# Three rings of buffers around the feed-forward up products of a one-core transformer layer

## The chip, the cores and the metric

The kernel runs on one core of a Trainium2 chip. A core has TensorE (PE in the profile, its weight loads PEld), VectorE (DVE), ScalarE (ACT), GpSimd (POOL) and SyncE (SP), each with its own queue of instructions that it works through in order. The metric is the device time of one execution in microseconds; before and after are compared by their medians.

## The reference

One layer of a diffusion backbone on 2048 latent tokens and 128 context tokens, width 1024: modulated norm, an attention and a convolution branch, an output projection, and then a feed-forward part. Only the last one is touched here:

```python
def finish_layer(x, ao, co, gate_a, shift_f, scale_f, gate_f,
                 w_out, g_attn_post, g_ffn_pre, g_ffn_post, w_ffn_in, w_ffn_out):
    mix = jnp.concatenate([ao, co], axis=-1) @ w_out
    x = x + gate_a * rms_norm(mix, g_attn_post)
    u = rms_norm(x, g_ffn_pre) * (1.0 + scale_f) + shift_f
    gu = u @ w_ffn_in
    h = jax.nn.silu(gu[..., :D_FF]) * gu[..., D_FF:]
    return x + gate_f * rms_norm(h @ w_ffn_out, g_ffn_post)
```

D_FF is 2816, so `u @ w_ffn_in` is (2176 x 1024) by (1024 x 5632). The time before is 3061.99 us.

## The kernel before

**Up products.** The 17 row tiles of 128 tokens (16 latent, number 16 the context) are dealt into three chunks of 5, 6 and 6 tiles. The chunks are worked one after another, each over 22 blocks of the hidden width. One chunk and one block make a unit (`up_unit`): a Strassen-like scheme with seven products in place of eight, over pairs of row tiles. Each product takes 4 contraction steps, and each factor is split into a high and a low part, so a step is three matmuls (lines 957 to 959) and a unit 84, with 320 columns in chunk 0 and 384 in chunks 1 and 2.

**Weight operands.** For each unit two raw tiles of 512 KB are loaded (`wi_raw`, tag `t4`, four buffers). `wi_ops` forms four sums of quarter weights on GpSimd, each in a buffer `st` (line 919), and splits seven operands: ScalarE casts the high part (line 81), VectorE subtracts it for the low part (line 82). The split tiles `wi` lie in three `km` buffers and one `qt`, which come free as TensorE ends the products of the unit before. The sums follow one from another: s2 from s1, s4 from s2.

**Row operands.** The seven operands of chunk 0 (`u_ops`) are built ahead, during the output projection (`build_kept`), and kept. Those of chunks 1 and 2 are built in the middle of the chunk before (`build_spilled`), one pair of tiles after units 2, 8 and 14: six builds in all. `build_tile` loads a row tile `row` (line 834, tag `t4` as the raw weights), scales it on GpSimd (line 836), transposes it in eight matmuls (line 842) into PSUM banks of tag `c`, and copies these out on ScalarE (line 843). `build_pair` makes seven operands of two tiles, four of them by differences on GpSimd (`td`, line 860). Each is split into `hl` on ScalarE and VectorE and written to HBM (`u2d`, 512 KB). At the end of a chunk the operands of the next are read back (`u<-u2d`, 1.5 MB each); two of them already during the third build.

**What sets the order.** The instructions are traced in program order, and a scheduler puts them into one order for each engine, by a timeline of its own and by when buffers come free. So a ring of buffers that is longer also changes the order around it. All DMAs are issued from SP's queue. A tile's buffer is taken again when everything that reads it is done; for `hl` that is the landing of its write to HBM.

Of the kernel before, what the change touches and what calls it, by code (L numbers as in the profile page):

```python
# [8 lines left out]
F32 = mybir.dt.float32  # L9
F32R = mybir.dt.float32r  # L10
# [7 lines left out]
P = 128  # L18
D = 1024
# [21 lines left out]
def layer(ctx, tc, x_prompt, x_sample, cache_k, cache_v, cond, w_ada, b_ada, gcol,  # L41
# [28 lines left out]
    def dma(out, in_):  # L70

        out, in_ = (x.bitcast(F32) if x.dtype == F32R else x for x in (out, in_))
        with tc.issue_after(behind[0]) if behind else ExitStack():
            return nc.sync.dma_start(out, in_).ins
# [4 lines left out]
    def split(h, l, src, eng=None):  # L79

        S.copy(h, src)  # L81
        (eng or V).tensor_tensor(l, src, h.bitcast(F32), op=ALU.subtract)  # L82
# [20 lines left out]
    def pool(name, **kw):  # L103
        st = ExitStack()
        return st, st.enter_context(tc.tile_pool(name=name, reuse_waits="tile", **{"bufs": 1, **kw}))
# [574 lines left out]
    def t4(name):  # L680
        return prow.tile([P, D], F32, tag="t4", name=name, bufs=4)
# [142 lines left out]
    x_ex, bld = pool("extra", side="left")  # L824
# [6 lines left out]
    def build_tile(ti, bank):  # L831

        c = int(ti == 16)
        row = t4("row")
        dma(row, x2d[ti])
        G.tensor_scalar(row, row, r2s[:, ti:ti + 1], 1.0, op0=ALU.mult, op1=ALU.mult)
        ur = bld.tile([P, KT, P], F32, tag="ur", name="ur", bufs=2)
        for kk in range(2):
            up = bank().rearrange("p (a t) -> p a t", t=P)
            for a in range(4):  # L840
                kt = 4 * kk + a
                T.transpose(up[:, a, :], row[:, kt * P:(kt + 1) * P], ident)
                S.activation(ur[:, kt, :], up[:, a, :], AF.Identity, scale=modc[:, 2, c, kt:kt + 1],
                             bias=modc[:, 3, c, kt:kt + 1])
        return ur

    def build_pair(pair, bank, out):

        if len(pair) == 2:
            ua, ub_ = (build_tile(ti, bank) for ti in pair)  # L850
            w = P
        else:
            ur = build_tile(pair[0], bank)
            ua, ub_ = ur[:, :, 0:64], ur[:, :, 64:128]
            w = 64
        b11, b12, b21, b22 = ua[:, 0:4], ub_[:, 0:4], ua[:, 4:8], ub_[:, 4:8]

        def diff(x, y):
            t = bld.tile([P, 4, P], F32, tag="td", name="td", bufs=2)[:, :, :w]
            G.tensor_tensor(t, x, y, op=ALU.subtract)  # L860
            return t

        out(0, w, b11)
        out(3, w, b21)
        out(5, w, b22)
        t = diff(b12, b11)
        out(1, w, t)
        t2_ = diff(b22, t)
        out(2, w, t2_)
        out(6, w, diff(b21, t2_))  # L870
        out(4, w, diff(b22, b12))
# [38 lines left out]
    x_sm, sm_ = pool("small", side="right")  # L910
    x_ex, bld = pool("build", side="right")
    x_psg, psg = pool("psg", space=PSUM, bufs=2)

    def wi_ops(raws):
        a11, a12, a21, a22 = (r[:, i * 512:(i + 1) * 512] for r in raws for i in range(2))

        def total(x, y, op):
            t = sm_.tile([P, 512], F32, tag="st", name="st", bufs=2)
            G.tensor_tensor(t, x, y, op=op)  # L919
            return t  # L920

        dst = []
        for k in range(4):
            if k < 3:
                km = pk.tile([P, NALL], F32R, tag="km", name="wi", bufs=3)
                dst += [(km[:, 1024 * q:1024 * q + 512], km[:, 1024 * q + 512:1024 * q + 1024]) for q in range(2)]
            else:
                q = pk.tile([P, 2, 512], F32R, tag="qt", name="wi", bufs=2)
                dst.append((q[:, 0], q[:, 1]))
        split(*dst[0], a11)  # L930
        s1 = total(a21, a22, ALU.add)
        split(*dst[1], s1)
        s2 = total(s1, a11, ALU.subtract)
        split(*dst[2], s2)
        split(*dst[3], a12)
        s3 = total(a11, a21, ALU.subtract)
        split(*dst[4], s3)
        s4 = total(a12, s2, ALU.subtract)
        split(*dst[5], s4)
        split(*dst[6], a22)  # L940
        return dst
# [4 lines left out]
    def bank(tag):  # L946
        return psg.tile([P, 512], F32, tag=tag, name="psg")
# [51 lines left out]

    def build_spilled(c, k):  # L1000
        def out(i, w, src):
            hl = bld.tile([P, 2, 4, P], F32R, tag="hl", name="hl", bufs=1)
            split(hl[:, 0, :, :w], hl[:, 1, :, :w], src)
            dma(u2d[c, i][:, :, :, k * P:k * P + w], hl[:, :, :, :w])

        build_pair(chunks[c][k], lambda: bank("c"), out)
# [6 lines left out]
    for c in range(3):  # L1013
# [18 lines left out]
        elif c == 1:  # L1032
            u_ops = nxt + [u_load(pua, i, 2) for i in (2, 3)] + [u_load(pub, i, 2) for i in (4, 5, 6)]
            x_ex.close()
            x_ex, bld = pool("down", side="right")
# [33 lines left out]
    for gn, (c, g) in enumerate(groups):  # L1069
# [3 lines left out]
        for f in range(NF):  # L1073
# [9 lines left out]
            for i in range(len(tiles)):  # L1083
                hh, hl = (hhl[:, s, i * P:(i + 1) * P] for s in range(2))
# [75 lines left out]
```

## Time and profile before

| what | us |
|---|---|
| three runs | 3058.20, 3061.99, 3064.18 |
| median | 3061.99 |
| profiled execution, its time | 3067.98 |
| its span | 3066.2 |
| TensorE busy in the span | 2909.8 |
| chunk 0 of the up products | 1548 to 1862 |
| chunk 1 | 1862 to 2218 |
| chunk 2 | 2218 to 2538 |
| six builds of spilled operands | within 1594 to 2175 |

The profile's page gives busy time by engine, the chain of work that ended last, and groups of instructions by line with the idle time before them and what ended it. Other views give the same for a window, list who waited for whom, or show one tile's instructions. A wait is put down to what ended last.

### The profile page before, as it was taken

The numbers are of one execution on the slowest core, as the hardware profiler recorded it, in microseconds if no ns is written. First come the engines' busy times: TensorE is split into PE (matmuls) and PEld (weight loads), VectorE is DVE, ScalarE is ACT, GpSimd is POOL, SyncE is SP. The second block draws the span as 40 slices with busy tenths as digits, with TensorE's granted clock in tenths as the row PEclk, the third lists the DMA queues.
The fourth block names the chain that finished last, engine by engine and source line by source line (L and its number), as shares of the span: only waits on it lengthen the run. The fifth ranks groups of instructions, "written<-read, shape, count | busy, mean of one in ns | idle before, by whom it ended". The sixth has DMA issues, their size and how long they took to land. (4 is left out here: it accounts for less than half of the span.)

```text
span 3066.2 us, 47162 instructions
## 1 busy us (share of the span) xinstructions
PE 2909.8 (95%) x16925; PEld 2653.8 (87%) x16925; DVE 1994.7 (65%) x3824; ACT 1444.4 (47%) x2651; POOL 1230.1 (40%) x1114
## 2 busy tenths in 40 slices
PE   4999989999999999999999999999999999999998
PEld 3778879999999999988889988999999998788886
DVE  7899568787787887863366765556655554554443
ACT  3323236565565565664445553544444443444442
POOL 7313125554545544532245654555444440111110
PEclk7999999999999999999999999999999999999999
DMA  7777564454454454457645565444633235766663
GB/s 250 244 251 247 171 198 129 137 173 123 138 168 128 132 159 124 114 162 224 196 140 152 154 200 195 150 147 153 227 136 101 96 103 199 238 220 218 220 220 118
DMA packets 351180, 525.25 MB, mean 171 GB/s; under 512 B 33089, under 2 KB 264673, under 8 KB 349153
## 3 DMA queue, kind: packets, MB, share of 16 engines
q1 hardware_dynamic: 350944, 522.23, 53.7%
q8 instruction: 133, 2.18, 0.3%
q14 instruction: 103, 0.84, 0.1%
HBM read 393.79 MB, written 128.34 MB: 170 GB/s over the span
## 5 line engine op out<-in xcount | busy, mean ns | idle before, releaser
L957 PE MATMUL psg<-u,wi 128*128 128x384 f32 (+1 forms) x1848 | 606.6, 331 | 28.4 <-ACT wi L81 11.6
L959 PE MATMUL psg<-u,wi 128*128 128x384 f32 (+1 forms) x1848 | 597.6, 329 | 9.8 <-DVE wi L82 9.8
L958 PE MATMUL psg<-u,wi 128*128 128x384 f32 (+1 forms) x1848 | 606.2, 328 | 0.0
L505 DVE TENSOR_SCALAR_CACHE_REDUCE e<-s 128x436 f32<-128x436 f32 (+2 forms) x648 | 373.4, 600 | 87.1 <-PE s L502 70.7
L957 PEld LDWEIGHTS psg<-u,wi 128*128 128x128 f32 x1848 | 349.6, 190 | 38.6 <-ACT wi L81 15.5
L959 PEld LDWEIGHTS psg<-u,wi 128*128 128x128 f32 x1848 | 348.1, 189 | 13.9 <-DVE wi L82 13.5
L502 PE MATMUL s<-km,qt 128*128 128x436 f32 (+1 forms) x1280 | 344.1, 372 | 13.2 <-DVE e L505 9.1
L82 DVE TENSOR_TENSOR wi<-st,wi 128x512 fp32r<-128x512 f32 x264 | 246.1, 935 | 160.8 <-ACT wi L81 157.0
L958 PEld LDWEIGHTS psg<-u,wi 128*128 128x128 f32 x1848 | 350.1, 189 | 0.3
L82 DVE TENSOR_TENSOR wo<-rawo,wo 128x1024 fp32r<-128x1024 f32 x132 | 167.0, 1265 | 252.3 <-ACT wo L81 252.3
L510 ACT ACTIVATE e<-e,nm 128x2176 f32<-128x2176 f32 (+1 forms) x136 | 273.9, 2014 | 78.2 <-DVE nm L509 77.3
L81 ACT CAST wi<-st 128x512 fp32r<-128x512 f32 x264 | 163.3, 619 | 279.6 <-PE psg L959 190.8
L1089 PE MATMUL psy<-wo,hhl 128*128 128x512 f32 x748 | 286.0, 391 | 1.8 <-DVE hhl L82 1.8
L1088 PE MATMUL psy<-wo,hhl 128*128 128x512 f32 x748 | 286.5, 390 | 0.9 <-DVE wo L82 0.9
L1087 PE MATMUL psy<-wo,hhl 128*128 128x512 f32 x748 | 286.2, 391 | 0.0
L81 ACT CAST wo<-rawo 128x1024 fp32r<-128x1024 f32 x132 | 139.1, 1054 | 294.3 <-PE psy L1089 284.1
L82 DVE TENSOR_TENSOR wi<-raw,wi 128x512 fp32r<-128x512 f32 x198 | 233.0, 1193 | 35.5 <-ACT wi L81 30.7
L502 PEld LDWEIGHTS s<-km,qt 128*128 128x128 f32 x1280 | 209.1, 190 | 26.1 <-DVE e L505 17.5
L81 ACT CAST ath<-t 128x512 fp32r<-128x512 f32 (+2 forms) x292 | 157.4, 555 | 114.9 <-PE t L546 107.6
L82 DVE TENSOR_TENSOR atl<-t,ath 128x512 fp32r<-128x512 f32 (+2 forms) x292 | 187.1, 649 | 36.4 <-ACT ath L81 35.7
L1060 POOL TENSOR_TENSOR rr<-rr,mhalf 128x1 f32<-128x1 f32 x17 | 13.1, 779 | 452.7 <-DVE rr L1059 452.7
L919 POOL TENSOR_TENSOR st<-raw,st 128x512 f32<-128x512 f32 x66 | 87.3, 1322 | 254.4 <-DVE wi L82 254.4
(264 smaller groups left out, 7040.5 us busy)
## 6 DMA issues: line engine op xcount, KB each, us to landing
raw<-in_w_fi SPq DMA_DIRECT2D x132, 512.0 KB, 4.2
rawo<-in_w_fo SPq DMA_DIRECT2D x132, 512.0 KB, 3.6
fu<-ud SPq DMA_DIRECT2D x256, 256.0 KB, 4.7
raw<-in_w_ada SPq DMA_DIRECT2D x48, 512.0 KB, 5.2
u2d<-hl SPq DMA_DIRECT2D x42, 512.0 KB, 3.9
u<-u2d SPq DMA_DIRECT2D x14, 1536.0 KB, 10.7
hr<-hid SPq DMA_DIRECT2D x110, 192.0 KB, 3.5
hid<-hid SPq DMA_DIRECT2D x88, 192.0 KB, 3.6
```

The lines of the kernel that those rows point to most:

```text
L81: S.copy(h, src)
L82: (eng or V).tensor_tensor(l, src, h.bitcast(F32), op=ALU.subtract)
L502: mm = T.matmul(ps[:, :n], qt[:, s, m, t * P:(t + 1) * P], km[m][:, k0:k0 + n], start=(s == 0), stop=(s == 1))
L505: V.tensor_scalar(et[:, k0:k0 + n], ps[:, :n], SCALE, None, op0=ALU.mult, op1=ALU.max, accum_out=mx[:, ci:ci + 1])
L510: S.activation(et[:, :nk], et[:, :nk], AF.Exp, bias=nm, scale=1.0, accum_out=sm[:, t, m:m + 1])
L919: G.tensor_tensor(t, x, y, op=op)
L957: T.matmul(ps, h[:, ks], u[:, 0, kt, :n], start=start and kt == 0, stop=False, skip_group_check=not start)
L958: T.matmul(ps, h[:, ks], u[:, 1, kt, :n], start=False, stop=False, skip_group_check=not start)
L959: T.matmul(ps, l[:, ks], u[:, 0, kt, :n], start=False, stop=kt == 3, skip_group_check=not start)
L1087: T.matmul(banks[i][:, b, :], hh, woh_[:, bs], start=(f == 0), stop=False)
L1088: T.matmul(banks[i][:, b, :], hh, wol_[:, bs], start=False, stop=False)
L1089: T.matmul(banks[i][:, b, :], hl, woh_[:, bs], start=False, stop=(f == NF - 1))
```

## The change

Three allocations differ. The row tile gets a tag of its own in the pool of the builds, with one buffer, in place of one of the four `t4`. `st` has three buffers in place of two. `hl` has two in place of one. Every instruction stays, with the same sizes.

```diff
     def build_tile(ti, bank):

         c = int(ti == 16)
-        row = t4("row")
+        row = bld.tile([P, D], F32, tag="row", name="row")
         dma(row, x2d[ti])
...
         def total(x, y, op):
-            t = sm_.tile([P, 512], F32, tag="st", name="st", bufs=2)
+            t = sm_.tile([P, 512], F32, tag="st", name="st", bufs=3)
             G.tensor_tensor(t, x, y, op=op)
...
     def build_spilled(c, k):
         def out(i, w, src):
-            hl = bld.tile([P, 2, 4, P], F32R, tag="hl", name="hl", bufs=1)
+            hl = bld.tile([P, 2, 4, P], F32R, tag="hl", name="hl", bufs=2)
             split(hl[:, 0, :, :w], hl[:, 1, :, :w], src)
             dma(u2d[c, i][:, :, :, k * P:k * P + w], hl[:, :, :, :w])
```

The order moves on all engines from the first `build_tile` to the end of the builds. On ScalarE, in the second build of chunk 0, the fourth and fifth casts of `hl` stood like this before (`sg` and `u` are the gate's SiLU, `p` and `psg` copies of PSUM that the next products wait for):

```order
L81 CAST wi<-raw_19934 128x512
L81 CAST hl<-td 128x512
L976 ACTIVATE sg<-psg 128x320
L81 CAST wi<-st 128x512
L968 COPY psg<-psg 128x320
L983 ACTIVATE u_20020<-u_20020 128x320
L81 CAST wi<-st 128x512
L81 CAST wi<-raw_20071 128x512
L81 CAST hl<-td 128x512
```

and the fifth and sixth stand like this now:

```order
L971 COPY p_19965<-psg 128x320
L81 CAST wi<-st 128x512
L81 CAST hl<-td 128x512
L81 CAST wi<-raw_20069 128x512
L81 CAST hl<-td 128x512
L81 CAST wi<-st 128x512
L81 CAST wi<-raw_19934 128x512
```

Two casts of `hl` have one instruction between them instead of seven; the third and fourth of a build stand side by side. Counted in TensorE's matmuls that ScalarE's queue has waited for by then, the casts of tiles 3, 5 and 7 of a build lie 35 and 24 apart in chunk 0 (first and third build), and 21 and 39 in chunk 1 (first and second build).

On SP, around the loads of the row tiles for the second build of chunk 0 (x2d_119 and x2d_111 are the rows of tiles 16 and 8), before:

```order
L74 DMA row<-x2d_119 128x1024
L74 DMA hid_7_16913<-hid 128x256
L74 DMA hid_7_16913<-hid 128x64
L74 DMA row<-x2d_111 128x1024
L74 DMA hid_7_16913<-hid 128x256
L74 DMA hid_7_16913<-hid 128x64
L74 DMA raw_19795<-in_w_fi 128x1024
L74 DMA raw_19797<-in_w_fi 128x1024
```

Now x2d_119 is loaded during the build before it. x2d_111 comes within its own build, between the raw weights and the first writes of `hl`, and the first row of the next build (x2d_109) shortly behind it:

```order
L74 DMA u2d_18780<-hl 1024x1x128
...
L74 DMA raw_20069<-in_w_fi 128x1024
L74 DMA row<-x2d_111 128x1024
L74 DMA u2d_18783<-hl 1024x1x128
L74 DMA raw_20071<-in_w_fi 128x1024
L74 DMA row<-x2d_109 128x1024
L74 DMA u2d_18785<-hl 1024x1x128
L74 DMA u2d_18781<-hl 1024x1x128
```

Both rows stood ahead of the raw weights; now the second row of a pair is loaded when the first has been transposed. On TensorE the last transpose of the first row and the first of the second have 55, 41 and 55 matmuls of the products between them in the three builds of chunk 0, and 40, 36 and 60 in those of chunk 1.

## The prediction

> **What bounds the kernel now.** I read the page's busy line first, then stretches of the up products, then the waits of TensorE in the worst of them, then the tile that is named there.
>
> ```profile
> span 3066.2 us, 47162 instructions
> PE 2909.8 (95%) x16925; PEld 2653.8 (87%) x16925; DVE 1994.7 (65%) x3824; ACT 1444.4 (47%) x2651; POOL 1230.1 (40%) x1114
> ```
>
> TensorE is the bound: only what fills its 156 us of idle time, or what it waits for, can move the end. The change acts from the first rows built to the end of the up products, so I cut that part into stretches (window: length, PE busy with count, PEld, DVE, ACT, POOL, clock, DMA share, GB/s):
>
> ```profile
> 1380.00:1545.00 165.00, 165.00 (x746) 135.37 (x745) 58.90 (x81) 75.96 (x180) 38.16 (x47) 1.00 0.65 202
> 1594.08:1654.04 59.96, 53.60 (x351) 50.74 (x350) 42.52 (x48) 31.97 (x68) 34.28 (x24) 1.00 0.61 178
> 1679.15:1738.67 59.52, 53.75 (x350) 52.09 (x349) 44.02 (x49) 31.36 (x67) 34.34 (x24) 0.97 0.61 179
> 1763.66:1824.80 61.14, 54.91 (x352) 52.29 (x350) 40.61 (x49) 32.02 (x68) 34.45 (x24) 0.97 0.71 221
> 1824.80:1849.44 24.64, 24.64 (x171) 24.64 (x169) 16.18 (x20) 12.02 (x25) 13.71 (x10) 1.00 0.39 119
> 1899.84:1968.45 68.61, 63.26 (x354) 59.65 (x353) 41.51 (x50) 34.75 (x73) 36.62 (x27) 1.00 0.53 158
> 1997.57:2080.14 82.57, 77.94 (x437) 75.76 (x437) 50.93 (x57) 40.11 (x83) 42.95 (x30) 0.98 0.48 145
> 2094.70:2174.25 79.55, 75.96 (x437) 74.32 (x437) 50.94 (x59) 41.36 (x86) 43.27 (x30) 1.00 0.64 198
> 2174.25:2217.93 43.68, 43.68 (x253) 43.68 (x253) 25.10 (x32) 18.50 (x36) 20.61 (x15) 1.00 0.54 193
> 2217.93:2538.00 320.07, 320.07 (x1848) 320.07 (x1848) 174.31 (x219) 136.37 (x263) 146.31 (x108) 1.00 0.35 116
> ```
>
> Rows 2 to 4 are the three builds of spilled operands in chunk 0, rows 6 to 8 those in chunk 1; rows 5 and 9 are units without a build, the last is chunk 2, which builds nothing. Without a build TensorE never pauses, and the pace is 24.64/171 = 0.144 us a matmul in chunk 0 and 43.68/253 = 0.173 us in chunk 1. At that pace the six builds would take 50.6, 50.4, 50.7, 61.1, 75.4 and 75.4 us. They take 9.4, 9.1, 10.4, 7.5, 7.1 and 4.1 us more: **47.6 us**, the most that this change can take from its own stretches. The first row, with the kept operands, has no idle time, so nothing is to be won there. TensorE's waits from 1594 to 2175 us:
>
> ```profile
> PE psg L957 <- ACT psg L968: 9.1, 10, 1.7
> PE psg L959 <- DVE wi L82: 8.9, 12, 1.6
> PE psg L957 <- ACT wi L81: 8.7, 8, 3.2
> ```
>
> These three, 26.7 us, are a copy and splits that ACT and DVE deliver late. The tile hl says why they are late:
>
> ```profile
> L81 ACT CAST hl<-td x24: 617/622/625, 1621.3 to 2162.0; 128x512 fp32r<-128x512 f32 x24
> L82 DVE TENSOR_TENSOR hl<-td,hl x24: 675/692/1785, 1622.4 to 2162.7; 128x512 fp32r<-128x512 f32 x24
> ...
>   DMA u2d<-hl: 75.7, 29
> ...
> DMA to landing us min/median/max: 3.5/3.9/10.4
> ```
>
> With one buffer each cast of hl waits until the tile before it has landed in HBM: a cycle of 0.62 + 0.69 + 3.9 = 5.2 us, in which ACT, which works in order, does nothing else. It stood 75.7 us at these casts. One such wait, on ACT and then on TensorE:
>
> ```profile
> 1783.53 0.62 ACT L81 CAST wi<-st 128x512 fp32r<-128x512 f32 x1 [0.54 <-POOL st L919]
> 1790.95 0.62 ACT L81 CAST hl<-ur 128x512 fp32r<-128x512 f32 x1 [6.80 <-DMA u2d<-hl]
> 1791.48 0.42 ACT L971 COPY p<-psg 128x320 f32<-128x320 f32 x1
> 1791.79 0.62 ACT L81 CAST wi<-raw 128x512 fp32r<-128x512 f32 x1
> ...
> 1792.47 0.42 PE L957 MATMUL psg<-u,wi 128*128 128x320 f32 x1 [3.23 <-ACT wi L81]
> ```
>
> The weight cast that TensorE wants stands behind the hl cast; it comes 6.8 us late and TensorE stops for 3.2 us. After some stops the clock falls too:
>
> ```profile
> 1711.00:1717.90 6.90, 4.73 (x33) 4.46 (x31) 5.24 (x6) 3.19 (x7) 6.20 (x5) 1.00 0.85 258
> 1717.94:1721.35 3.41, 3.41 (x13) 3.33 (x14) 3.41 (x4) 2.08 (x5) 2.09 (x3) 0.50 0.56 158
> 1721.35:1724.76 3.41, 3.41 (x25) 3.41 (x24) 2.31 (x3) 1.00 (x2) 1.42 (x1) 1.00 0.40 112
> ```
>
> 13 matmuls instead of 25 in 3.41 us: about 1.6 us are lost each time, and this belongs to the 47.6. Here 6.90 - 4.73 = 2.2 us of idle time in the stretch ahead sufficed for it.
>
> **The change part by part.** No instruction is added or removed; three rings of buffers and the order differ.
>
> *Second hl buffer.* Cast k now waits for the landing of tile k-2. In the new order tiles 3 and 4 go side by side, and 5 and 6 follow. Counted in matmuls, tile 5 stands 35 behind tile 3 in chunk 0 (35 x 0.144 = 5.0 us, needed 5.2: held 0.2 us) and tile 7 stands 24 behind tile 5 (3.5 us: held 1.7). In chunk 1 it is 21 (3.6 us: held 1.6) and 39 (6.7 us: nothing held). That is 1.9 and 1.6 us a build, 10 us for six. In the third build of each chunk 1.5 MB operand loads share the DMA engines and a landing took up to 10.4 us, 6.5 more than the median; I keep one of these for each of the two, 13 us. So ACT is held 23 us in place of 75.7, 30%, and if TensorE's loss falls alike, 14 to 15 of the 47.6 us stay: **-33 us**. Bounds: all of it (-47.6), or, if landings go to 10.4 us throughout, a cycle of 11.7 us against those spacings: 6.7 + 8.2 us a build in chunk 0 and 8.1 + 5.0 in chunk 1, 84 us held as before, gain 0.
>
> *Own tile for the row, and third st.* What they touch:
>
> ```profile
> L919 POOL TENSOR_TENSOR st<-raw 128x512 f32<-128x512 f32 x38 | 58.0, 1525 | 22.4 <-DMA raw<-in_w_fi 20.9
> L919 POOL TENSOR_TENSOR st<-raw,st 128x512 f32<-128x512 f32 x38 | 50.8, 1338 | 94.1 <-DVE wi L82 94.1
> ...
> L836 POOL TENSOR_SCALAR row<-row,r2s x11: 1122/1492/2088, 1590.1 to 2101.9; 128x1024 f32<-128x1024 f32 x11
> ...
> DMA to landing us min/median/max: 3.1/3.5/4.5
> ```
>
> POOL's fourth sum waits 94.1 us for DVE, as the two st are taken; the third ends that wait. Raw weights no longer share t4 with rows, so the 20.9 us of waits for them should shrink. Chunk 2 runs with two st and no pause, so neither binds TensorE outside the builds, and inside they work through the same late splits: cost 0 by themselves, between -6 (part of the 8.9 us on DVE's splits) and the loss of the second rival. What the row pays: its second tile loads only after the first is transposed. Between the two sets of transposes the new order has 55, 41, 55 matmuls in chunk 0 and 40, 36, 60 in chunk 1, so 7.9, 5.9, 7.9, 6.9, 6.2 and 10.4 us, for a landing of 3.5 and a scaling of 1.5: 5.0 us, covered by 0.9 to 5.4 us. For the kept operands the same serial load lies under projection matmuls with no idle time: 0.
>
> **Sum.** 3066.2 - 33 = 3033.2 us of span, and with the 1.8 us that the profiled execution has around it 3035. Its own time, 3067.98, is 6.0 us above the median 3061.99, so the forecast for a median is **3029 us**.
>
> **The rivals.**
> *Landings still pace the casts* (0.20). For it: pairs of 512 KB writes go out together, beside raw loads, and a landing without any operand load has taken 6.65 us already:
>
> ```profile
> 1629.46 6.65 DMA u2d<-hl
> ```
>
> Then the cycle is 8.0 us, the holds 3.0 + 4.5 us a build in chunk 0 and 4.4 + 1.3 in chunk 1, 40 for six, 53 with the operand loads: 70% of 75.7 stay, gain 14, 3048 us. Against it: DMA is busy 0.48 to 0.71 of the builds.
> *The second row comes late* (0.08), the slower side. The first transposes of the second row stand in TensorE's order; behind them everything waits. The scaling stands on POOL behind a sum that waits for DVE. At 6 us for that wait, the path is 3.5 + 6 + 1.3 + 1.5 = 12.3 us against the spacings above: short by 4.4, 6.4, 4.4, 5.4, 6.1 and 1.9, 28.6 us, and six half-clock spells of 1.6 bring 38. Against the gain of 33 that is 5 slower, 3067. It decides from a mean lateness of 3.9 us (6 x (3.9 + 1.6) = 33). Against it: the fourth sum waits only 94.1/38 = 2.5 us, and the third st is what shortens this.
> *DVE and POOL in each other's way* (0.05). DVE's subtraction takes 0.69 us in the median and up to 1.79 (row of hl). If the freed POOL made all seven splits of a chunk 0 unit take 1.79, they need 12.5 us of the unit's 12.1 (84 x 0.144) before any other DVE work; with 1.4 us of PSUM reads 13.9, 1.8 over, times 22 units 40 us, less the gain 7 slower: 3069. It decides from (12.1 - 1.4)/7 = 1.53 us a split. The splits and one of the three reads:
>
> ```profile
> L82 DVE TENSOR_TENSOR wi<-st,wi 128x512 fp32r<-128x512 f32 x171 | 176.5, 1036 | 83.7 <-ACT wi L81 80.5
> ...
> L979 DVE TENSOR_TENSOR c<-psg,p 128x320 f32<-128x320 f32 x22 | 10.6, 483 | 3.1 <-PE psg L959 2.4 <-ACT p L971 0.7
> ```
>
> The mean of 1.04 us is far from 1.53. The Trainium skill (SBUF — State Buffer, SBUF: two separate sides) calls the port of the two engines an exclusive lock, held for the whole instruction when DVE reads two SBUF operands; the trace agrees in kind, 0.69 alone and up to 1.79, but POOL's amount of work stays the same.
> *The buffers change nothing* (0.05): the order already shows two hl casts side by side, so only if the late splits had another cause. 3060.
>
> **How the numbers follow.** Forecast 0.62, gain 20 to 47 us, 3015 to 3042. The first rival, 3048 with some 7 us either way, reaches 3055; a full recovery (47.6) and 5 us of the waits outside the builds, where raw weights also share t4, end at 3009. What lies outside is the slower cases and half of no change: range 3009 to 3056. A change of 0.2%, 6 us, is about what can be told from none. Faster: the forecast, the first rival, and 0.02 of the row case where lateness is smaller than the gain, 0.84. Same: 0.05 and some 0.02 of rivals that just cancel, 0.07. Slower: 0.09.
>
> **What would show it.** ACT's wait for u2d<-hl falls from 75.7 us to about 23 and the six stretches lose some 33 us of their 47.6; POOL's wait for DVE at the fourth sum all but goes. TensorE's wait for POOL's row (L842 <- row L836) stays near 0; if it shows 10 us or more the row rival is at work. DVE's mean at wi above 1.2 us would show the port. The forecast fails if ACT's hold falls and TensorE's idle time does not.

## The result, and the profile after

| | median us | runs | range |
|---|---|---|---|
| before | 3062.06 | 8 | 3058.20 to 3066.70 |
| after | 3080.94 | 8 | 3071.69 to 3088.87 |

The ratio is 1.0056, with a 95% interval of 1.0043 to 1.0070: the change makes the kernel **slower by 0.56%**, where 1.1% faster was forecast, 3029 us with a range of 3009 to 3056. The profiled execution after took 3071.69 us, the fastest of its eight, so its trace shows less of the loss than the median has.

The page of the changed kernel, its first two lines:

```profile
span 3069.9 us, 47302 instructions
PE 2907.6 (95%) x16925; PEld 2655.4 (86%) x16925; DVE 1944.0 (63%) x3824; ACT 1437.3 (47%) x2651; POOL 1236.8 (40%) x1114
```

VectorE is busy for less time in total than before (1944.0 us against 1994.7), and ScalarE no longer stands at the casts of hl. The view of that tile after:

```profile
L82 DVE TENSOR_TENSOR hl<-td,hl x24: 676/1492/1779, 1614.3 to 2160.2; 128x512 fp32r<-128x512 f32 x24
...
  DMA u2d<-hl: 4.6, 7
...
DMA to landing us min/median/max: 3.4/3.9/9.3
```

The hold of 75.7 us is 4.6 us now, far below the 23 us of the forecast. But the median subtraction of an operand takes 1.49 us in place of 0.69. The waits of TensorE in the same stretch as before, 1594 to 2175 us (engine and what waited, for whom: us, times, longest):

```profile
PE psg L957 <- DVE c L979: 16.3, 5, 4.3
PE psg L959 <- DVE wi L82: 7.0, 6, 4.1
PE psg L957 <- ACT wi L81: 6.9, 11, 1.5
PE psg L957 <- ACT sg L976: 6.8, 3, 4.6
PE psg L842 <- POOL row L836: 3.8, 4, 1.4
```

ScalarE's copies (9.1 us before) have all but left the list, and a new name leads it: VectorE's reading of PSUM, c, with 16.3 us in five waits. The six builds, each from the end of the unit behind which it stands (window: length, PE, PEld, DVE, ACT, POOL, clock, DMA share, GB/s), and below them two units without a build and chunk 2:

```profile
1589.14:1640.28 51.14, 43.69 (x264) 41.09 (x263) 31.34 (x36) 26.10 (x56) 29.97 (x20) 0.93 0.58 171
1677.81:1728.15 50.34, 42.05 (x266) 40.02 (x264) 30.46 (x37) 27.11 (x57) 30.96 (x21) 0.93 0.58 174
1765.77:1812.76 46.99, 40.40 (x264) 38.11 (x263) 31.65 (x37) 27.36 (x58) 31.51 (x21) 1.00 0.78 247
1895.97:1966.36 70.39, 63.53 (x354) 61.27 (x354) 43.18 (x50) 34.58 (x73) 41.01 (x28) 0.98 0.55 170
1995.60:2064.72 69.12, 63.35 (x352) 61.62 (x352) 39.54 (x47) 33.47 (x70) 37.99 (x26) 0.95 0.50 153
2093.96:2164.91 70.95, 63.58 (x353) 61.09 (x352) 40.48 (x47) 35.12 (x73) 35.29 (x25) 0.98 0.55 179
1640.28:1665.03 24.75, 24.75 (x171) 24.75 (x170) 16.69 (x22) 11.47 (x25) 16.23 (x11) 1.00 0.42 130
2223.15:2543.60 320.45, 320.45 (x1850) 320.45 (x1850) 150.90 (x219) 132.86 (x263) 141.86 (x106) 1.00 0.33 116
```

At the pace of the prediction (0.144 and 0.173 us a matmul) the builds would take 38.0, 38.3, 38.0, 61.2, 60.9 and 61.1 us; they take 13.1, 12.0, 9.0, 9.2, 8.2 and 9.9 more, **61 us in place of 47.6**. Length less PE busy is 42.3 us of idle time, where the six rows quoted before give 31.9. Units without a build and chunk 2 run as they did. Chunks 0 and 1 together take 10 us longer (1543.5 to 2223.1 us, before 1548.3 to 2217.9). In this trace they also start 4.8 us earlier, so the span grows by 3.7 us only.

Before, the longest stops of the six builds were 1.3, 2.2, 3.2, 1.6, 1.7 and 1.7 us. Now they are 3.5, 4.6, 3.5, 4.3, 4.3 and 4.2 us. The first, in TensorE's timeline:

```profile
1624.23 0.47 PE L957 MATMUL psg<-u,wi 128*128 128x320 f32 x1 [3.52 <-DVE c L979]
```

and what VectorE did ahead of it, in its own:

```profile
1614.32 1.57 DVE L82 TENSOR_TENSOR hl<-td,hl 128x512 fp32r<-128x512 f32 x1
1615.92 0.49 DVE L979 TENSOR_TENSOR c<-psg,p 128x320 f32<-128x320 f32 x1
1616.33 0.48 DVE L982 TENSOR_TENSOR u<-psg,p 128x320 f32<-128x320 f32 x1
1616.73 0.70 DVE L82 TENSOR_TENSOR wi<-st,wi 128x512 fp32r<-128x512 f32 x1
1617.35 1.78 DVE L82 TENSOR_TENSOR wi<-raw,wi 128x512 fp32r<-128x512 f32 x1
1619.06 1.78 DVE L82 TENSOR_TENSOR wi<-st,wi 128x512 fp32r<-128x512 f32 x1
1620.77 1.34 DVE L82 TENSOR_TENSOR hl<-td,hl 128x512 fp32r<-128x512 f32 x1
1622.03 1.74 DVE L82 TENSOR_TENSOR wi<-st,wi 128x512 fp32r<-128x512 f32 x1
1623.70 0.48 DVE L979 TENSOR_TENSOR c<-psg,p 128x320 f32<-128x320 f32 x1
```

None of these rows has idle time ahead of it. TensorE has nothing left from 1620.7 us; the read of PSUM that it needs stands behind five splits, four of which take 1.34 to 1.78 us. Four of the six long stops wait for c in this way. The other two lead to VectorE's queue as well: the second waits for the gate's SiLU on ScalarE, which waits for a read of PSUM (hid) that VectorE does late, and the sixth for a split of weights:

```profile
1715.95 0.64 PE L957 MATMUL psg<-u,wi 128*128 128x320 f32 x1 [4.64 <-ACT sg L976]
1715.46 0.44 ACT L976 ACTIVATE sg<-psg 128x320 f32<-128x320 f32 x1 [4.25 <-DVE hid L988]
2153.17 0.45 PE L959 MATMUL psg<-u,wi 128*128 128x384 f32 x1 [4.15 <-DVE wi L82]
```

GpSimd during the first stop:

```profile
1612.11 1.52 POOL L860 TENSOR_TENSOR td<-ur 128x512 f32<-128x512 f32 x1 [2.16 <-ACT ur L843]
1613.60 1.74 POOL L919 TENSOR_TENSOR st<-raw,st 128x512 f32<-128x512 f32 x1
1615.32 1.57 POOL L836 TENSOR_SCALAR row<-row,r2s 128x1024 f32<-128x1024 f32 x1
1616.86 3.43 POOL L860 TENSOR_TENSOR td<-ur,td 128x512 f32<-128x512 f32 x2
1620.26 1.30 POOL L985 TENSOR_TENSOR hid<-u,c 128x320 f32<-128x320 f32 x1
1621.52 1.70 POOL L919 TENSOR_TENSOR st<-raw 128x512 f32<-128x512 f32 x1
1623.19 1.72 POOL L860 TENSOR_TENSOR td<-ur 128x512 f32<-128x512 f32 x1
```

From the first difference on it works without a pause as well: all four differences of the build fall within 13 us. The first of them waits until 1612.11 us for ScalarE's copies of transposed rows: the second row is scaled only at 1603.17 us, and its last transposes end at 1610.7.

After such a stop the granted clock is at half for a while. The stretch ahead of the restart and the one behind it:

```profile
1617.33:1624.23 6.90, 3.38 (x24) 3.11 (x23) 6.90 (x7) 4.31 (x8) 6.82 (x5) 1.00 0.71 206
1624.23:1627.64 3.41, 3.41 (x13) 3.41 (x14) 3.41 (x5) 1.41 (x3) 3.41 (x3) 0.53 0.63 171
```

13 matmuls in 3.41 us, where some 24 fit at full clock. By the timed runs most of the loss is of this kind. Every run has its span and its mean granted clock; as an estimate, their product is the time that it would take at full clock, and the rest is lost to the lower one. For the eight runs after, the mean is 3016 us at full clock and 63 us lost; for the kernel before (four sets of 13 to 28 runs, beside the experiments) 3011 to 3014 and 47 to 49. The clock is given to 0.001, 3 us of a span, so a mean of eight is good to a microsecond or two. Of some 19 us, 14 to 16 are then lost clock and 2 to 5 are work that ends later. The slowest run after has a clock of 0.977, the fastest 0.983: 71 and 52 us lost, 19 of difference where 17 lie between the two runs. The two traced executions can't show this share: both have a mean clock of 0.983. In chunks 0 and 1 the half-clock time rises from 20.5 to 30.7 us, 5 us of lost time, and the rest of the span made up for it in that execution. The clock fell during or behind five of the six long stops, not at the one at 1800 us. The Trainium skill (TensorE: Matmul & The Clock Gate, Why this matters for your kernels) advises against idle gaps of more than about 3 us. All six are above that; the row quoted before, with 2.2 us of idle time in 6.9, shows that less can do.

### The profile page after: what moved, and what is told of

It is laid out like the page before. It is cut to its first block, busy times and chain, and to the rows that moved or that the text cites. A ratio compares the mean times of both kernels' runs of the same rounds, so it can differ in the third digit from the quotient of the medians.

```text
span 3069.9 us, 47302 instructions
## 1 busy us (share of the span) xinstructions
PE 2907.6 (95%) x16925; PEld 2655.4 (86%) x16925; DVE 1944.0 (63%) x3824; ACT 1437.3 (47%) x2651; POOL 1236.8 (40%) x1114
## 4 chain that ended last, share of the span: by engine, by line
PE 74%; DVE 9%; issue 6%; DMA 5%; POOL 3%; ACT 2%; SPq 1%; DVEq 0%; POOLq 0%; ACTq 0%
PE psg L957 9%; PE psg L959 9%; PE psg L958 9%; PE s L502 7%; PE psy L1089 4%; PE psy L1087 4%; PE psy L1088 4%; PE t L546 3%; PE pq L239 2%; PE pq L237 2%; PE pq L238 2%; PE psx L725 2%; PE psx L726 2%; PE psx L724 2%; PE o L539 2%
## 5 line engine op out<-in xcount | busy, mean ns | idle before, releaser
L957 PE MATMUL psg<-u,wi 128*128 128x384 f32 (+1 forms) x1848 | 608.0, 332 | 38.2 <-DVE c L979 17.7
L82 DVE TENSOR_TENSOR wi<-st,wi 128x512 fp32r<-128x512 f32 x264 | 206.4, 801 | 179.7 <-ACT wi L81 179.0
L82 DVE TENSOR_TENSOR wi<-raw,wi 128x512 fp32r<-128x512 f32 x198 | 197.8, 1014 | 44.6 <-ACT wi L81 36.5
L1060 POOL TENSOR_TENSOR rr<-rr,mhalf 128x1 f32<-128x1 f32 x17 | 13.1, 779 | 451.3 <-DVE rr L1059 451.3
L919 POOL TENSOR_TENSOR st<-st,raw 128x512 f32<-128x512 f32 x66 | 106.8, 1618 | 198.5 <-issue 178.7
```

The costliest lines, as they stand in the source:

```text
L957: T.matmul(ps, h[:, ks], u[:, 0, kt, :n], start=start and kt == 0, stop=False, skip_group_check=not start)
```

## Experiments: one part, two parts

The first question was whether one of the three parts does the harm. Each kernel is the kernel before with one of the edits, or two. Ratios are to the kernel before on the same chip.

**Second hl alone.**

```diff
-            hl = bld.tile([P, 2, 4, P], F32R, tag="hl", name="hl", bufs=1)
+            hl = bld.tile([P, 2, 4, P], F32R, tag="hl", name="hl", bufs=2)
```

> The kernel before with the second hl buffer alone. Theory A (with the waits for hl gone, the builds' work on POOL and DVE crowds together, DVE's subtractions take twice as long beside POOL, and TensorE makes one long stop a build): ACT's wait for u2d<-hl falls from 75.7 us below 15, DVE's hl subtraction goes from 0.69 us in the median towards 1.3 or more, stops of 3 us and more appear in most builds, and the time is 3065 to 3085 us. Theory B (the freed sums and the row's own tile are what crowds POOL; hl alone is good): stops of 3 us and more stay rare and the time is 3025 to 3045 us.

Measured: 3054.76 us, 0.9978 (0.9966 to 0.9991), between the two ranges. The part that carried the forecast gains 0.2% and not 1.1%. The signs of theory A are there in part: two builds have a stop of 3.3 us, and the median subtraction of a difference takes 1.38 us. ScalarE's hold falls from 75.7 to 14.4 us, but TensorE's idle time in the builds only from 31.9 to 24.3 us, and VectorE's c has become the longest wait here already:

```profile
PE psg L957 <- DVE c L979: 9.8, 6, 3.3
PE psg L957 <- ACT psg L968: 7.8, 8, 2.9
```

**Own row tile alone.**

```diff
-        row = t4("row")
+        row = bld.tile([P, D], F32, tag="row", name="row")
```

> The kernel before with the row's own tile alone. Theory A: hl still paces the builds, so no new long stops, 3056 to 3068 us. Theory C (the second row of a pair comes late and TensorE stands before its transposes): waits of TensorE for POOL's row of 5 us or more in total, 3068 to 3085 us.

Measured: 3055.65 us, 0.9982 (0.9970 to 0.9994), just below theory A's range. The serial load of the second row stops TensorE by itself almost nowhere (1.1 us of waits for GpSimd's row at the transposes): the rival of the second row, as it was priced, is out.

**Third st alone.**

```diff
-            t = sm_.tile([P, 512], F32, tag="st", name="st", bufs=2)
+            t = sm_.tile([P, 512], F32, tag="st", name="st", bufs=3)
```

> The kernel before with the third st alone. Theory A: 3050 to 3064 us, since hl still paces the builds and the sums come earlier. Theory B (freed sums crowd POOL beside DVE): DVE's mean at wi rises above 1.15 us in the up products' first two chunks, 3066 to 3085 us.

Measured: 3068.91 us, 1.0022 (1.0013 to 1.0032). A longer ring loses by itself. ScalarE still stands 73.3 us at hl, and TensorE waits 11.4 us for c (2.8 before, 1543 to 2225 us). The time lies in theory B's range, but its sign is missing: the mean split of weights is 0.95 us (of sums) and 1.06 us (of raw quarters), below the 1.04 and 1.18 of the kernel before. Why this ring alone costs 0.2% stays open.

**The pairs**, each as the two diffs above together: row and hl, st and hl, row and st.

> The row's own tile and the second hl buffer, st with two buffers as before. Theory A1 (the third st lets POOL run without a pause; only with it does the crowding cost more than the waits for hl did): the two gains of 0.2% add up, 3040 to 3056 us. Theory A2 (row and hl together already crowd the builds): 3062 to 3085 us, with stops of 3 us and more in most builds.

> The third st and the second hl buffer, the row in t4 as before. Theory A1: worse than the sum of the two alone (which would be 3060 us), 3066 to 3085 us, with stops of 3 us and more in most builds. Theory A2: the sum, 3052 to 3064 us.

> The row's own tile and the third st, hl with one buffer as before. Theory A (either form: hl still paces the builds): the sum of the two alone, 3056 to 3068 us. Theory E (the row's tile and the third st spoil each other, through the order of raw loads and rows, without hl): 3070 to 3085 us.

Measured: row and hl 3059.36 us, 0.9989 (0.9977 to 1.0001); **st and hl 3043.72 us, 0.9938 (0.9923 to 0.9953)**; row and st 3062.43 us, 0.9996 (0.9986 to 1.0005). Row and st came as expected; row and hl lies between its two ranges, and st and hl 8 us below both of its own. The kernel of st and hl ran once more, beside other kernels:

> The kernel of e6 again, row in t4, three st and two hl. If e6's 0.9938 is the kernel's own: 0.992 to 0.9955 of the kernel before, with one long stop or none apart from those for the operands' loads. If it was luck of the half-clock spells: 0.996 to 1.000.

Measured: 3044.52 us, 0.9937 (0.9916 to 0.9959), so it is the kernel's own.

No part is to blame by itself, and the parts do not add: the product of the three ratios is 0.9982, and the three together give 1.0056. Any two of them give no loss; the row's own tile, which alone gains 0.2%, costs 1.2% on top of st and hl (1.0056 against 0.9938). Nor does the time follow ScalarE's hold at hl: it is 19.2 us with st and hl, 4.5 with row and hl, 40.8 with row and st, and 4.6 in the changed kernel, the slowest of them.

## Experiments: is it crowding on VectorE and GpSimd

**Without the differences.** The changed kernel, but the four operands of a build that are differences are made of one term each; the differences are left out, and nothing else.

```diff
         def diff(x, y):
-            t = bld.tile([P, 4, P], F32, tag="td", name="td", bufs=2)[:, :, :w]
-            G.tensor_tensor(t, x, y, op=ALU.subtract)
-            return t
+            return x
```

> The changed kernel without the four differences on POOL in each build (operands 1, 2, 4 and 6 are copies of row operands, so those products are others; the kept operands too). DVE's order stays nearly the same. Theory A (DVE's subtractions are slow because POOL works beside them): DVE's hl subtraction falls from 1.49 us in the median below 1.0, the stops of 3.5 to 4.6 us go or fall below 2 us, and the time is 3025 to 3050 us. Theory D (the order alone: the reads of PSUM stand too deep behind splits in DVE's queue): stops stay at 3 us and more and the time is 3065 to 3085 us.

Measured: 3057.66 us, 0.9989 (0.9976 to 1.0002), 0.7% below the changed kernel and between the ranges of the two theories. Every split and every PSUM read is still there. What is gone are 24 operations of GpSimd in the builds, and with them most of the wait for c, and all but two of the stops of over 2.5 us (lines are two less in this kernel):

```profile
PE psg L957 <- DVE wi L82: 10.5, 10, 2.7
PE psg L955 <- DVE c L977: 7.2, 6, 1.4
```

**Operands spread over four units.** The changed kernel, but a build is worked in four steps behind four units in turn, with the casts behind the gate's SiLU on ScalarE and the differences behind the gate product on GpSimd.

```diff
-            up_unit(c, f, ws, u_ops)
...
-                build_spilled(c + 1, f // 6)
+            done_marks = up_unit(c, f, ws, u_ops)
...
+                with tc.issue_after(done_marks[0]), tc.issue_after(done_marks[1]):
+                    next(steps, None)
```

> The changed kernel, but the operands of a build are made over four units instead of about two and a half: after units 2, 3, 4 and 5 of each six one, two, two and two operands, with the casts held on ACT behind that unit's SiLU and the differences held on POOL behind that unit's gate product. Theory A (crowding of POOL and DVE is what stops TensorE): the stops of 3.5 to 4.6 us go, half-clock time in the first two chunks falls from 30.7 us below 20, and the time is 3025 to 3055 us. Theory D (the order of DVE's queue, not the load): stops stay, 3065 to 3085 us.

Measured: 3056.6 us, 0.9978 (0.9966 to 0.9989), 2 us above theory A's range and 0.8% below the changed kernel with the same buffers and the same work. TensorE's wait for c is gone from the list of its waits, no stop exceeds 2.5 us in the builds, and the clock is never at half in chunks 0 and 1. The subtractions of operands are as slow as before:

```profile
L82 DVE TENSOR_TENSOR hl<-td,hl x24: 680/1314/1787, 1632.5 to 2160.1; 128x512 fp32r<-128x512 f32 x24
```

So a slow split does not stop TensorE by itself. It does where several stand back to back ahead of a read of PSUM that is due. Their number alone does not tell, though three expectations below go by it: between two reads of PSUM the traces have up to 13 splits in the changed kernel and in the one without differences, and 12 in this one. The 13 of the changed kernel's first build stand ahead of the read at 1615.92 us, with pauses of up to 5.5 us among them; the stop comes later, behind five without a pause.

## Experiments: why the row's own tile hurts beside the other two

In the changed kernel the next pair's first row is scaled in the middle of the differences (at 1615.32 us in GpSimd's rows above). The first theory was that these 1.6 to 2.0 us are what is too much.

**Scaling held back.** The changed kernel, with the scaling behind the gate product of the unit behind which the build stands.

```diff
-        G.tensor_scalar(row, row, r2s[:, ti:ti + 1], 1.0, op0=ALU.mult, op1=ALU.mult)
+        with tc.issue_after(unit_marks[1]) if unit_marks else ExitStack():
+            G.tensor_scalar(row, row, r2s[:, ti:ti + 1], 1.0, op0=ALU.mult, op1=ALU.mult)
...
-            up_unit(c, f, ws, u_ops)
+            unit_marks = up_unit(c, f, ws, u_ops)
```

> The change, with one difference: GpSimd's scaling of the next row is held behind the gate product of the unit after which the build stands, so it lies ahead of the burst of differences and sums and not among them. Theory R (the next row's scaling, 1.6 to 2.0 us in the middle of the burst, is what makes st+hl, 0.9938, into the change, 1.0056): 3043 to 3060 us, stops of over 2.5 us fall from 6 to 2 or less, half-clock time from 30.7 us to under 14. Rival T (with its own tile the row no longer takes one of the four t4, raw weights come earlier, and their sums and splits fall into the builds): where the scaling stands changes little, 3068 to 3085 us, four or more long stops.

**Scaling on ScalarE.**

```diff
-        G.tensor_scalar(row, row, r2s[:, ti:ti + 1], 1.0, op0=ALU.mult, op1=ALU.mult)
+        S.activation(row, row, AF.Copy, scale=r2s[:, ti:ti + 1])
```

> The change, with the rows scaled on ScalarE in place of GpSimd: 12 operations of 1.5 us leave GpSimd in the builds. Theory R: near e9, 3043 to 3060 us, long stops mostly gone. Rival T: 3068 to 3085 us, with four or more long stops. A third possibility: a row that waits on ScalarE for its landing holds the copies behind it, then TensorE waits for ACT's psg and p by 10 us more than in the change.

Measured: held back 3085.31 us, 1.0077 (1.0062 to 1.0093); on ScalarE 3073.37 us, 1.0037 (1.0024 to 1.0050), in rival T's range or just above it. Holding back does more than was meant: both rows of a pair are scaled behind the gate product, and the seven subtractions of a build then fall within 27 to 36 us, in the changed kernel within 38 to 49. So the second kernel is the better test. Both still have six stops of over 2.5 us (on ScalarE two of these are at the transposes), and with no row on GpSimd at all the wait for c is longer than in the changed kernel:

```profile
PE psg L957 <- DVE c L979: 20.5, 6, 4.9
PE psg L842 <- ACT row L836: 8.5, 5, 3.1
```

**This theory fell.** Two were left: (S) with one buffer for the rows, the second row of a pair comes late, and everything that needs both rows falls into one burst; (T) rows outside t4 leave four buffers to the raw weights, whose sums and splits then run ahead into the builds.

**Mixed: only the first row of a pair has the own tile**, the second one takes a t4 and need not wait for the first.

```diff
-        row = bld.tile([P, D], F32, tag="row", name="row")
+        row = bld.tile([P, D], F32, tag="row", name="row") if own else t4("row")
...
-            ua, ub_ = (build_tile(ti, bank) for ti in pair)
+            ua, ub_ = (build_tile(ti, bank, ti == pair[0]) for ti in pair)
```

> The change, but of a pair of rows only the first has the tile of its own; the second takes one of the four t4 as before, so that it need not wait for the first. In VectorE's order the most splits of weights and operands between two reads of PSUM in a build are 9 to 7, in the change 13. Theory S (the second row comes late, and the operands then fall into one burst): 3030 to 3050 us, near st+hl (0.9938), no stop of over 2.5 us apart from those at the operands' loads, half-clock time under 14 us. Rival T (raw weights run ahead when rows don't share t4; here one of two rows still does): between st+hl and the change, 3055 to 3070 us.

**Three t4**, with one own tile for the rows, and **three t4 with two own tiles** for the rows; the second differs from the first only in the last diff.

```diff
-        return prow.tile([P, D], F32, tag="t4", name=name, bufs=4)
+        return prow.tile([P, D], F32, tag="t4", name=name, bufs=3)
```

```diff
-        row = bld.tile([P, D], F32, tag="row", name="row")
+        row = bld.tile([P, D], F32, tag="row", name="row", bufs=2)
```

> The change with three t4 in place of four: the rows still have one tile of their own and the second row comes late, but raw weights are held back. VectorE's order has 13 splits between two reads of PSUM in five builds and 12 in one. Theory S: slow as the change, 3065 to 3095 us, with four long stops or more. Rival T: faster than the change by 0.8% or more, 3035 to 3058 us. If three t4 are too few outside the builds, chunk 2, 320 us without a pause so far, gets longer; that would be seen apart from this.

> The change with two buffers for the rows and three t4: both rows of a pair can be loaded early, raw weights have three buffers. VectorE's order has at most 9 splits between two reads of PSUM in a build. Theory S: 3030 to 3050 us, few long stops. Rival T: also faster than the change, 3035 to 3058 us; e14 beside it then tells. If neither holds: above 3065 us.

Measured: **mixed 3036.15 us, 0.9907 (0.9892 to 0.9922)**, three t4 3073.07 us, 1.0028 (1.0019 to 1.0038), three t4 with two row tiles 3047.01 us, 0.9942 (0.9925 to 0.9959). The three times lie within the bounds of theory S, and the first two outside those of T. Not all signs came as forecast: the mixed kernel has one stop of 2.8 us in a build, and of the four long stops of three t4 only two are in a build. The cleanest pair is the last: one more buffer for the rows, raw weights alike, and 0.86% of the time goes (0.9942 against 1.0028). The mixed kernel, the fastest of all, has ScalarE standing 24.1 us at hl, the changed one 4.6.

T is not nothing. Three t4 cost both kernels a stop at the start of chunk 0, where the raw weights come late; in the kernel with one row tile:

```profile
1565.26 0.64 PE L957 MATMUL psg<-u,wi 128*128 128x320 f32 x1 [9.54 <-ACT wi L81]
```

In the builds alone, this kernel has 30.9 us of idle time against 42.3 in the changed one, and with two row tiles it is 14.9, as in the mixed kernel (15.3). So of 27 us, holding back the raw weights can stand for 11, or the other order that comes with it; the second row's coming early, with the order that it brings, stands for 16. How far the two are one thing wasn't settled.

TensorE's waits of the mixed kernel over the first two chunks (1543 to 2225 us), where the changed one has 17.7 us for c, 8.8 for DVE's wi and 8.3 for ACT's wi:

```profile
PE psg L957 <- DVE c L979: 8.4, 7, 2.2
PE psg L959 <- DVE wi L82: 5.1, 3, 2.8
PE psg L957 <- ACT wi L81: 3.8, 4, 1.5
```

and GpSimd in its first build:

```profile
1606.09 1.13 POOL L836 TENSOR_SCALAR row<-row,r2s 128x1024 f32<-128x1024 f32 x1 [3.10 <-DMA row<-x2d]
1607.18 1.30 POOL L919 TENSOR_TENSOR st<-raw 128x512 f32<-128x512 f32 x1
1608.44 1.30 POOL L860 TENSOR_TENSOR td<-ur 128x512 f32<-128x512 f32 x1
1612.46 1.62 POOL L919 TENSOR_TENSOR st<-st,raw 128x512 f32<-128x512 f32 x1 [2.73 <-issue]
1614.05 1.74 POOL L919 TENSOR_TENSOR st<-raw,raw 128x512 f32<-128x512 f32 x1
1615.76 1.74 POOL L860 TENSOR_TENSOR td<-ur,td 128x512 f32<-128x512 f32 x1
...
1621.19 1.58 POOL L860 TENSOR_TENSOR td<-ur,td 128x512 f32<-128x512 f32 x1 [0.69 <-DVE hl L82]
...
1627.02 1.61 POOL L860 TENSOR_TENSOR td<-ur 128x512 f32<-128x512 f32 x1 [1.30 <-DVE hl L82]
```

The row scaled at 1606.09 belongs to the next pair; both rows of this one were ready before. The first difference comes 12.4 us after the first subtraction of an operand (1596.08), in the changed kernel 20.0 (1592.15 to 1612.11), and the four of them are spread over 20 us with sums and idle moments between, where the changed kernel has them within 13. The kernel before has its first difference no earlier (1613.8 us), but spreads the four over 20 us too. A short burst alone doesn't make a stop: with st and hl the differences of a build take 11 to 18 us, and no stop in a build exceeds 2.5 us. How the late second row turns into the stops is read from these timelines; no run shows that step by itself.

**Spreading with the rows in t4**, as a last version: the spread kernel with `row = t4("row")`.

```diff
-        row = bld.tile([P, D], F32, tag="row", name="row")
+        row = t4("row")
```

> Operands made over four units as in e8, with three st and two hl, but the row in t4 as before. If the spreading alone is what helps, near e8: 3053 to 3060 us. If the row's place in t4 helps as it did between the change and st+hl, and adds to it: 3035 to 3045 us. If rows in t4 now hold back raw weights for longer, since a build lasts four units: above 3062 us.

Measured: 3050.52 us, 0.9959 (0.9947 to 0.9970): better than spreading with the own tile (0.9978), not as good as st and hl without spreading (0.9938). The guess of 3035 to 3045 us was too low.

All kernels together: the median's ratio, the idle time of TensorE in units 2 to 18 of chunks 0 and 1 (one profile each; the second one of st and hl gives 17.7), and for the timed runs the mean of span times clock and of what the clock lost.

| kernel | ratio | idle in builds | at full clock | lost to clock |
|---|---|---|---|---|
| before | 1 | 31.9 | 3011 to 3014 | 47 to 49 |
| hl | 0.9978 | 24.3 | 3001 | 51 |
| row | 0.9982 | 22.5 | 3004 | 50 |
| st | 1.0022 | 34.6 | 3013 | 54 |
| row, hl | 0.9989 | 23.3 | 3005 | 52 |
| st, hl (first time) | 0.9938 | 18.3 | 2995 | 47 |
| row, st | 0.9996 | 29.9 | 3010 | 50 |
| all three: the change | 1.0056 | 42.3 | 3016 | 63 |
| change without differences | 0.9989 | 26.7 | 3007 | 48 |
| change, spread | 0.9978 | 26.2 | 3012 | 44 |
| spread, row in t4 | 0.9959 | 22.4 | 3005 | 44 |
| change, scaling held back | 1.0077 | 43.4 | 3028 | 56 |
| change, scaling on ScalarE | 1.0037 | 36.3 | 3010 | 62 |
| mixed | 0.9907 | 15.3 | 2990 | 44 |
| three t4, one row tile | 1.0028 | 30.9 | 3011 | 59 |
| three t4, two row tiles | 0.9942 | 14.9 | 2990 | 56 |

The change and the change with its operands spread differ by 5 us at full clock and by 19 in what the clock loses: there the difference lies in the clock and not in the work, and the spread kernel is the one without long stops. The mixed kernel beats both, the kernel before by 0.93% and the change by 1.5%.

## Why the prediction failed, step by step

**What bounds the kernel, and the 47.6 us to be had: right.** Units without a build and chunk 2 did not move, and the mixed kernel takes some of exactly this time: its idle time in the builds is 15.3 us where the kernel before has 31.9.

**ScalarE's hold: right in direction, too cautious in size.** 23 us were forecast to stay of 75.7; 4.6 us did. The first rival (landings still pace the casts, 0.20) is out: the landings have the same median of 3.9 us.

**"If TensorE's loss falls alike": this step failed first.** It took ScalarE's hold for the cause of the stops and let TensorE gain in proportion. With hl alone the hold fell by 61 us (81%) and TensorE's idle time in the builds by 7.6 us (24%). The wait was also a spacing: one cast of an operand every 5.2 us at most kept the operands apart on VectorE and the differences apart on GpSimd. Without it they come closer together, the subtractions of differences go from 0.69 to 1.38 us in the median, and VectorE's c (9.8 us) stands ahead of ScalarE's copy (7.8 us) among what TensorE waits for. The prediction's last sentence names this case (the hold falls and TensorE's idle time does not), but it had no chance of its own.

**"Own tile for the row, and third st: cost 0 by themselves": this step decided the sign.** By themselves they are worth -0.18% and +0.22%. The step asked whether the second row is in time for its transposes, and it nearly is: TensorE waits 3.8 us for GpSimd's row at L842, where the rival of the second row (0.08) was to show 10 us or more. It did not ask what is late behind the transposes. Every difference needs the second row, and without the other waits all four fall into 13 us. As we read it, one hl still paces the casts by landings (row and st: 0.9996), two st the sums by VectorE (row and hl: 0.9989), and an early second row the differences (st and hl: 0.9938); the change takes away all three spacings at once. The ratios are measured, the three names for what paces are an inference. That the row's part decides is shown by the mixed kernel (0.9907) and by the pair with three t4. The third st did not do what this step gave it for either: GpSimd's wait for VectorE at the fourth sum, which was to go, is 64.9 us in place of 94.1, and over all four sums it is 126.1 in place of 117.6.

**DVE and POOL in each other's way (0.05): the nearest of the rivals, and wrong in its measure.** It looked at the mean split over whole units: 1.53 us were needed, and VectorE's mean at wi fell (the page has wi<-st at 935 ns before and 801 after). The harm is done by a few splits in a row of 1.3 to 1.8 us ahead of what TensorE needs next. The sign by which it was to be known, a mean over 1.2 us, could not show that. That the two engines slow each other is borne out in part only: without the differences the wait for c falls from 17.7 to 7.2 us, but splits of 1.79 us remain, beside the sums.

**The clock: counted, but with the wrong sign.** The prediction had half-clock spells inside the 47.6 us and saw that 2.2 us of idle time in 6.9 suffice for one, but let them shrink with the stops. They grew: by the estimate above 14 to 16 of the 19 us are this term. Theories that call the change harmless in sum (buffers change nothing, 0.05) are out by the interval.

## What to carry to other kernels

A wait that an engine spends on a buffer can be what keeps the next engines from being crowded: before it is removed, write down what will then come back to back on the engine that reads PSUM, and add up the time, not the number, of what stands ahead of each such read. Judge rings of buffers together and by the order that they bring, since here two of three gained up to 0.6% and the third turned this into a loss. For a row, a tile or a load that becomes serial, look not only at its first reader but at everything that needs the last one.

## What was not expected of the hardware

- Idle time in total does not tell what it costs in clock. In chunks 0 and 1 the kernel before has 42.6 us of idle time and 20.5 us at half clock, the change 50.9 and 30.7, the spread kernel 33.9 and none at all, with no stop above 2.4 us. But a stop of 2.2 us in the kernel before (at 1717.8 us) was followed by a spell, and one of 3.5 us in the change (at 1800.3) was not. In these chunks a spell lasted 3.41 or 6.83 us, and 10.24 us during and behind the stops of 9.5 and 8.1 us in the kernels with three t4.
- One subtraction of 128x512 on VectorE with both operands in SBUF took from 0.68 to 1.83 us, with GpSimd at work beside it in the long cases that are quoted. With GpSimd's differences gone, operand splits still went up to 1.79 us, as the sums of weights remain.
